# Batched x·yᵀ on one core: 2 MB stores and 64-column weight tiles, with a last tile cut into unequal partition ranges

## The chip, the cores and the metric

The kernel runs on one core of a Trainium2 chip. Its time is the device time in microseconds (us), as the median of the runs shown. The core has TensorE (PE in the profile; PEld is its weight load), VectorE (DVE), ScalarE (ACT), GpSimd (POOL), SyncE (SP, which here only issues transfers), and sixteen DMA engines that move data between the device memory and SBUF. Matrix products are written to PSUM, and an engine has to copy them to SBUF before a transfer can store them.

## The reference

```python
def setup_inputs():
    batch, n_heads, seq_t, seq_s, channels = 8, 12, 512, 512, 64
    return {
        "x": np.random.randn(batch, n_heads, seq_t, channels).astype(np.float32),
        "y": np.random.randn(batch, n_heads, seq_s, channels).astype(np.float32),
    }

def reference(x, y):
    return np.einsum('bhtc,bhsc->bhts', x, y).astype(np.float32)
```

For each of the 96 pairs of batch and head, `out = x @ y.T`: 512 x 64 times 64 x 512, in float32. The inputs are 2 x 12.6 MB and the output is 100.7 MB, so most of the traffic is the store of the output.

## The kernel before

Four heads make a group (`G = 4`), and there are `NG = 24` groups. A partition of a group holds 16 consecutive rows of one head (`R = 16`), 32 partitions a head (`Q = 32`). So a group's x or y is one contiguous block of 512 KB with 4 KB a partition, and its output is one contiguous block of 4 MB with 32 KB a partition.

`load(g)` (L48 to L53) issues the transfers of y and x for a group on SyncE's queue. Six groups are loaded ahead, and group g + 6 is asked for when group g is cast. `prepare(g)` (L61 to L93) is a generator that makes a group's operands, in four steps:

- GpSimd casts y and x to bf16 (L65, L69). y is written twice side by side, so that its transposes fill both halves of the partitions. The loads of group g + 6 are issued here.
- TensorE transposes eight blocks of y into PSUM (L78), and VectorE copies them to `yT` (L84). The copy reads PSUM with a stride, so that the columns of `yT` stand in the order of the rows of y.
- The other eight blocks follow, copied by ScalarE (L86).
- TensorE transposes x in eight blocks of two rows a partition (L90), and VectorE copies the result to `xT` as it lies (L91).

The main loop (L98 to L123) goes over the groups. For each it has eight steps k, and at every second one it takes one step of `prepare(g + 1)`. A step multiplies two rows of each partition: one PSUM tile `pm` of 128 partitions x 2 x 512, filled by eight matmuls (L109): four heads times two parities of the row (`par`). Each has 64 contraction rows and 32 weight columns, so the eight use eight separate blocks of the 128 x 128 array, two in height and four in width. ScalarE copies the even steps' `pm` to the output tile `ot` (L116), VectorE the odd ones' (L118). There are three `pm` buffers and four `ot` buffers of 4 MB.

A group's 4 MB leave in one transfer (L123), except for the first and the last group, which leave in four pieces of 1 MB (L121), each as soon as its two steps are done. All loads and stores are issued by SyncE, in the order of the program; the framework gives each a semaphore from a ring of eight. An `ot` buffer is written again only after its store has landed.

Of the kernel before, what the change touches and what calls it, by code (L numbers as in the profile page):

```python
# [1 line left out]

# [5 lines left out]


@with_exitstack  # L10
def kernel(
    ctx: ExitStack,
    tc: tile.TileContext,
    x: bass.AP,
    y: bass.AP,
    out: bass.AP,
):

    nc = tc.nc
    B, H, T, C = x.shape
    _, _, S, _ = y.shape
    P = 128
    G = 4
    Q = P // G
    R = T // Q
    NG = B * H // G
    K = R // 2
    fp32 = mybir.dt.float32  # L30
    bf16 = mybir.dt.bfloat16
    assert C * 2 == P and S == T and R == 16

    xv = x.rearrange("b h t c -> (b h t c)").rearrange("(g p n) -> g p n", p=P, n=R * C)
    yv = y.rearrange("b h t c -> (b h t c)").rearrange("(g p n) -> g p n", p=P, n=R * C)
    ov = out.rearrange("b h t s -> (b h t s)").rearrange("(g p n) -> g p n", p=P, n=R * S)

    const = ctx.enter_context(tc.tile_pool(name="const", bufs=1))
    lpool = ctx.enter_context(tc.tile_pool(name="lpool", bufs=6))
    bpool = ctx.enter_context(tc.tile_pool(name="bpool", bufs=2))  # L40
    tpool = ctx.enter_context(tc.tile_pool(name="tpool", bufs=2))
    opool = ctx.enter_context(tc.tile_pool(name="opool", bufs=4))
    ptpool = ctx.enter_context(tc.tile_pool(name="ptpsum", bufs=2, space=bass.MemoryType.PSUM))
    pmpool = ctx.enter_context(tc.tile_pool(name="pmpsum", bufs=3, space=bass.MemoryType.PSUM))

    loaded = {}

    def load(g):  # L48
        xs = lpool.tile([P, R * C], fp32)
        ys = lpool.tile([P, R * C], fp32)  # L50
        nc.sync.dma_start(ys, yv[g])
        nc.sync.dma_start(xs, xv[g])
        loaded[g] = (xs, ys)  # L53

    for g in range(6):
        load(g)

    ident = const.tile([P, P], bf16)
    make_identity(nc, ident)

    def prepare(g, made):  # L61

        xs, ys = loaded.pop(g)
        yb = bpool.tile([P, R, 2, C], bf16)
        nc.gpsimd.tensor_copy(  # L65
            yb, ys.rearrange("p (r c) -> p r c", c=C).unsqueeze(2).to_broadcast([P, R, 2, C])
        )
        xb = bpool.tile([P, R * C], bf16)
        nc.gpsimd.tensor_copy(xb, xs)  # L69
        if g + 6 < NG:  # L70
            load(g + 6)
        yield
        yT = tpool.tile([P, G * Q, R], bf16)
        xT = tpool.tile([P, K, P], bf16)
        for half in range(2):
            pt = ptpool.tile([P, K, P], bf16)
            for k in range(K):
                nc.tensor.transpose(  # L78
                    pt[:, k, :], yb[:, half * K + k].rearrange("p a c -> p (a c)"), ident
                )  # L80
            dst = yT[:, :, half * K:(half + 1) * K]
            src = pt.rearrange("p k n -> p n k")
            if half == 0:
                nc.vector.tensor_copy(dst, src)  # L84
            else:
                nc.scalar.activation(dst, src, mybir.ActivationFunctionType.Copy)  # L86
            yield
        pt = ptpool.tile([P, K, P], bf16)
        for k in range(K):
            nc.tensor.transpose(pt[:, k, :], xb[:, k * P:(k + 1) * P], ident)  # L90
        nc.vector.tensor_copy(xT, pt)  # L91
        made[g] = (xT, yT.rearrange("p n k -> p (n k)"))
        yield  # L93

    made = {}
    for _ in prepare(0, made):
        pass
    for g in range(NG):  # L98
        xT, yT = made.pop(g)
        steps = prepare(g + 1, made) if g + 1 < NG else iter(())  # L100
        ot = opool.tile([P, R, S], fp32)
        edge = g == 0 or g == NG - 1
        for k in range(K):
            if k % 2 == 0:
                next(steps, None)
            pm = pmpool.tile([P, 2, S], fp32)
            for h in range(G):
                for par in range(2):
                    nc.tensor.matmul(  # L109
                        pm[h * Q:(h + 1) * Q, par, :],  # L110
                        xT[par * C:(par + 1) * C, k, h * Q:(h + 1) * Q],
                        yT[par * C:(par + 1) * C, h * S:(h + 1) * S],
                        start=True, stop=True,
                    )
            if k % 2 == 0:
                nc.scalar.activation(ot[:, 2 * k:2 * k + 2, :], pm, mybir.ActivationFunctionType.Copy)  # L116
            else:
                nc.vector.tensor_copy(ot[:, 2 * k:2 * k + 2, :], pm)  # L118
            if edge and k % 2 == 1:
                a, b = (2 * k - 2) * S, (2 * k + 2) * S  # L120
                nc.sync.dma_start(ov[g][:, a:b], ot.rearrange("p r s -> p (r s)")[:, a:b])  # L121
        if not edge:
            nc.sync.dma_start(ov[g], ot.rearrange("p r s -> p (r s)"))  # L123


# [1 line left out]
_INS = ['x', 'y']  # L127
_OUTS = [((8, 12, 512, 512), 'float32')]


# [23 lines left out]
```

## Time and profile before

| | |
|---|---|
| Time, median of 3 runs | 309.21 us (309.09 to 309.28) |
| Profiled execution: time, span of its instructions | 309.28 us, 307.5 us |
| TensorE busy (matmuls) | 158.3 us, 51% |
| VectorE busy | 157.3 us, 51% |
| ScalarE busy | 119.1 us, 39% |
| GpSimd busy | 70.6 us, 23% |
| DMA: moved, mean rate | 126.14 MB, 410 GB/s |
| Instructions | 4865 |
| A 4 MB store, issue to landing (median) | 36.6 us |

The DMA share in the profile is the mean over the sixteen DMA engines: 1.00 when all are busy, 0.06 when one of sixteen is. Figures slightly above 1.00 come from packets whose records overlap a little at their ends. q1 is the queue that SyncE's transfers use, and q8 carries instruction code. In the answers by stretches, each engine has its busy time and, in brackets, its number of instructions. In the waits of SyncE's queue, each line has the waiting line, what ended the wait, the total in us, how many times and the longest. In the groups of instructions, the numbers after the count are the busy time in us and the mean duration in ns, then the idle time before them and what ended most of it.

The trace also has, for every transfer, sixteen landing times, one for each DMA engine that moved a part of it, without the engine's number. A 128-partition transfer is cut in sixteen parts of eight partitions, each partition's contiguous run being one packet.

### The profile page before, as it was taken

Reading aid. Unit: us, or ns where it says so; the run is one execution under the profiler, and the core shown is the slowest. Engines: PE = TensorE matmul, PEld = TensorE weight load, DVE = VectorE, ACT = ScalarE, POOL = GpSimd, SP = SyncE. Lnnn points to the kernel's source line nnn. Section 1 sums busy time; section 2 is a strip of 40 time slices with the busy share of each in tenths; the row PEclk is TensorE's granted clock in tenths of the full one; section 3 lists DMA queues with packets and bytes.
Section 4 is the critical chain, followed back from the end, with each engine's and each line's share of the span. In section 5 each row is a group of like instructions: output and inputs, shape, how many; then the busy total and the mean of one; then the engine's idle time right before and its main releaser. Section 6 shows DMA issues by size and latency. Waiting matters only on the chain.

```text
span 307.5 us, 4865 instructions
## 1 busy us (share of the span) xinstructions
PE 158.3 (51%) x2112; PEld 81.2 (26%) x2112; DVE 157.3 (51%) x144; ACT 119.1 (39%) x121; POOL 70.6 (23%) x54
## 2 busy tenths in 40 slices
PE   2877775483564735648447474383754854320000
PEld 2443342341322313224133241231413412000000
DVE  0599997275373643736537356373563775340000
ACT  1587856144162341623506336053261564330000
POOL 5863354132122221222212312132121000000000
PEclk9999998556655667575575755757555575555555
DMA  7999999999999999999999999999999999999970
GB/s 288 417 376 425 449 405 462 412 427 435 415 436 429 404 450 420 432 436 409 448 426 404 457 420 413 451 412 443 428 431 431 437 431 420 439 432 426 410 302 21
DMA packets 11253, 126.14 MB, mean 410 GB/s; under 512 B 1248, under 2 KB 1248, under 8 KB 7392
## 3 DMA queue, kind: packets, MB, share of 16 engines
q1 hardware_dynamic: 11232, 125.83, 96.7%
q8 instruction: 16, 0.26, 0.3%
q14 instruction: 5, 0.04, 0.0%
HBM read 25.17 MB, written 100.66 MB: 409 GB/s over the span
## 4 chain that ended last, share of the span: by engine, by line
DMA 72%; DVE 11%; PE 2%; issue 1%; ACT 1%; POOL 1%; SPq 0%; DVEq 0%; ACTq 0%
DMA out_dram<-ot 71%; DVE ot L118 8%; DVE yT L84 2%; PE pm L109 1%; DMA ys<-in_y_dram 1%; ACT ot L116 1%; DVE xT L91 1%; PE pt L78 1%; POOL yb L65 1%; PE pt L90 0%; ACT yT L86 0%; SPq L123 0%; DVEq L118 0%; ACTq L116 0%
## 5 line engine op out<-in xcount | busy, mean ns | idle before, releaser
L118 DVE COPY ot<-pm 128x1024 f32<-128x1024 f32 x96 | 114.8, 1221 | 91.0 <-DMA out_dram<-ot 77.2
L116 ACT ACTIVATE ot<-pm 128x1024 f32<-128x1024 f32 x96 | 96.0, 1023 | 143.9 <-DMA out_dram<-ot 121.2
L109 PE MATMUL pm<-yT,xT 64*32 64x512 bf16 x1536 | 98.0, 555 | 100.6 <-ACT ot L116 84.0
L109 PEld LDWEIGHTS <-xT 64*32 64x32 bf16 x1536 | 30.0, 96 | 156.2 <-issue 142.9
L65 POOL CAST yb<-ys 128x2048 bf16<-128x2048 f32 x24 | 45.5, 1896 | 96.9 <-DMA ys<-in_y_dram 79.6
L78 PE MATMUL pt<-ident,yb 128*128 128x128 bf16 x384 | 42.8, 278 | 7.2 <-POOL yb L65 6.1
L69 POOL CAST xb<-xs 128x1024 bf16<-128x1024 f32 x24 | 25.0, 1042 | 65.1 <-PE pt L90 65.1
L78 PEld LDWEIGHTS <-yb 128*128 128x128 bf16 x384 | 35.5, 131 | 15.5 <-issue 7.8
L84 DVE COPY yT<-pt 128x1024 bf16<-128x1024 bf16 x24 | 29.2, 1215 | 7.2 <-PE pt L78 7.2
L90 PE MATMUL pt<-ident,xb 128*128 128x128 bf16 x192 | 26.4, 284 | 5.6 <-ACT yT L86 4.9
L86 ACT ACTIVATE yT<-pt 128x1024 bf16<-128x1024 bf16 x24 | 24.5, 1019 | 8.6 <-PE pt L78 8.6
L91 DVE COPY xT<-pt 128x1024 bf16<-128x1024 bf16 x24 | 16.6, 690 | 17.5 <-PE pt L90 17.5
L90 PEld LDWEIGHTS <-xb 128*128 128x128 bf16 x192 | 16.9, 127 | 18.1 <-issue 18.1
L86 ACT ACT_TABLE_LOAD x1 | 1.3, 1283 | 0.7 <-PEq L138 0.7
masks.py:199 POOL TENSOR_SCALAR_AFFINE_SELECT ident<-ident 128x128 bf16<-128x128 bf16 x1 | 0.3, 294 | 0.1
masks.py:197 POOL MEMSET ident<- 128x128 bf16 x1 | 0.2, 205 | 0.3 <-POOLq L138 0.3
L138 POOL MEMSET const-float32-0.0<- 128x1 f32 x1 | 0.1, 99 | 0.2 <-issue 0.2
L138 POOL MEMSET const-bfloat16-1.0<- 128x1 bf16 x1 | 0.1, 102 | 0.0
L138 POOL MEMSET const-uint8-127<- 128x1 uint8 x1 | 0.1, 102 | 0.0
L138 POOL MEMSET const-float32-1.0<- 128x1 f32 x1 | 0.1, 99 | 0.0
## 6 DMA issues: line engine op xcount, KB each, us to landing
out_dram<-ot SPq DMA_DIRECT2D x22, 4096.0 KB, 36.6
ys<-in_y_dram SPq DMA_DIRECT2D x24, 512.0 KB, 35.7
xs<-in_x_dram SPq DMA_DIRECT2D x24, 512.0 KB, 27.3
out_dram<-ot SPq DMA_DIRECT2D x8, 1024.0 KB, 23.6
```

Of the source, the lines that this page charges most:

```text
L65: nc.gpsimd.tensor_copy(yb, ys.rearrange("p (r c) -> p r c", c=C).unsqueeze(2).to_broadcast([P, R, 2, C]))
L69: nc.gpsimd.tensor_copy(xb, xs)
L78: nc.tensor.transpose(pt[:, k, :], yb[:, half * K + k].rearrange("p a c -> p (a c)"), ident)
L84: nc.vector.tensor_copy(dst, src)
L86: nc.scalar.activation(dst, src, mybir.ActivationFunctionType.Copy)
L90: nc.tensor.transpose(pt[:, k, :], xb[:, k * P:(k + 1) * P], ident)
L91: nc.vector.tensor_copy(xT, pt)
L109: nc.tensor.matmul(pm[h * Q:(h + 1) * Q, par, :], xT[par * C:(par + 1) * C, k, h * Q:(h + 1) * Q], yT[par * C:(par + 1) * C, h * S:(h + 1) ...
L116: nc.scalar.activation(ot[:, 2 * k:2 * k + 2, :], pm, mybir.ActivationFunctionType.Copy)
L118: nc.vector.tensor_copy(ot[:, 2 * k:2 * k + 2, :], pm)
L138: nc = _bacc.Bacc("TRN2", target_bir_lowering=False, num_devices=1)
```

## The change

The output is split in halves of a group: `HP = 2` heads a tile, with 8 rows a partition (`I = 8`), 64 partitions a head. A tile is then 2 MB with 16 KB a partition, contiguous in the output as before. There are eight `ot` buffers of half the size, and two stores a group in place of one.

A weight tile has 64 columns in place of 32. The 64 partitions of a head are index q' = 2q + e, where q is one of the 32 partitions that the loaded x uses and e tells the first eight of its 16 rows from the last eight. To have these 64 columns side by side, the copy of the transposed x (L91) now writes `xT` with a stride of two elements, interleaving e. A `pm` takes four matmuls (two heads, two parities), and a group has 32 in place of 64. The copies of the transposed y are unchanged, and so are the number and size of the evictions.

Only the first tile and the last tile leave in pieces now. The first leaves in two pieces of 1 MB. The last is cut along the row into four ranges, and three of them are also cut along the partitions: columns of 6 KB a partition over 120 + 8 partitions, of 2 KB over all 128, of 3 KB over 108 + 20 and of 5 KB over 126 + 2, seven transfers in all.

```diff
+    HP = 2
+    I = R // 2
-    ov = out.rearrange("b h t s -> (b h t s)").rearrange("(g p n) -> g p n", p=P, n=R * S)
+    ov = out.rearrange("b h t s -> (b h t s)").rearrange("(g a p n) -> g a p n", a=G // HP, p=P, n=I * S)
...
-    opool = ctx.enter_context(tc.tile_pool(name="opool", bufs=4))
+    opool = ctx.enter_context(tc.tile_pool(name="opool", bufs=8))
...
-        xT = tpool.tile([P, K, P], bf16)
+        xT = tpool.tile([P, K // 2, P, 2], bf16)
...
-        nc.vector.tensor_copy(xT, pt)
+        nc.vector.tensor_copy(
+            xT.rearrange("p i n e -> p i e n"), pt.rearrange("p (e i) n -> p i e n", e=2)
+        )
...
-        ot = opool.tile([P, R, S], fp32)
-        edge = g == 0 or g == NG - 1
-        for k in range(K):
-            if k % 2 == 0:
-                next(steps, None)
-            pm = pmpool.tile([P, 2, S], fp32)
-            for h in range(G):
-                for par in range(2):
-                    nc.tensor.matmul(
-                        pm[h * Q:(h + 1) * Q, par, :],
-                        xT[par * C:(par + 1) * C, k, h * Q:(h + 1) * Q],
-                        yT[par * C:(par + 1) * C, h * S:(h + 1) * S],
...
+        for hp in range(G // HP):
+            ot = opool.tile([P, I, S], fp32)
+            edge = (g == 0 and hp == 0) or (g == NG - 1 and hp == 1)
+            for i2 in range(I // 2):
+                if i2 % 2 == 0:
+                    next(steps, None)
+                pm = pmpool.tile([P, 2, S], fp32)
+                for h2 in range(HP):
+                    h = hp * HP + h2
+                    for par in range(2):
+                        nc.tensor.matmul(
+                            pm[h2 * 64:(h2 + 1) * 64, par, :],
+                            xT[par * C:(par + 1) * C, i2, h * Q:(h + 1) * Q, :].rearrange("c q e -> c (q e)"),
+                            yT[par * C:(par + 1) * C, h * S:(h + 1) * S],
...
+                if edge and i2 % 2 == 1:
+                    otf = ot.rearrange("p r s -> p (r s)")
+                    if g == 0:
+                        cuts = [((2 * i2 - 2) * S, (2 * i2 + 2) * S, P)]
+                    elif i2 == 1:
+                        cuts = [(0, 3 * S, 120), (3 * S, 4 * S, P)]
+                    else:
+                        cuts = [(4 * S, 5 * S + S // 2, 108), (5 * S + S // 2, 8 * S, 126)]
+                    for a, b, n in cuts:
+                        nc.sync.dma_start(ov[g, hp][:n, a:b], otf[:n, a:b])
+                        if n < P:
+                            nc.sync.dma_start(ov[g, hp][n:, a:b], otf[n:, a:b])
+            if not edge:
+                nc.sync.dma_start(ov[g, hp], ot.rearrange("p r s -> p (r s)"))
```

## The prediction

> **What bounds the kernel now.** I read the page's slices and DMA queue first, then busy time in stretches, then the landing of every transfer on each of its sixteen DMA engines, then the queue of SyncE, and the compute groups last.
>
> The page, and its line on the queue that carries all loads and stores:
>
> ```profile
> DMA  7999999999999999999999999999999999999970
> ...
> q1 hardware_dynamic: 11232, 125.83, 96.7%
> q8 instruction: 16, 0.26, 0.3%
> ```
>
> The DMA engines are full from the second slice on, while no compute engine is above 51%. So an edit of compute is worth only what it does to the DMA engines, and what can be won lies in their 3.3% of idle time and in how evenly they end. The end, in stretches (columns: us, engines busy with instruction counts, clock, DMA share, GB/s):
>
> ```profile
> 237.20:247.40 10.20, 7.09 (x88) 3.67 (x88) 6.64 (x7) 4.90 (x5) 0.00 (x0) 0.57 1.01 432
> 257.40:267.50 10.10, 4.47 (x64) 1.25 (x64) 4.80 (x4) 3.99 (x4) 0.00 (x0) 0.50 0.99 423
> 267.50:277.40 9.90, 2.60 (x40) 0.75 (x39) 4.80 (x4) 3.99 (x4) 0.00 (x0) 0.50 1.00 431
> 277.40:287.10 9.70, 0.00 (x0) 0.00 (x0) 0.00 (x0) 0.00 (x0) 0.00 (x0) 0.50 0.98 424
> ...
> 297.00:300.20 3.20, 0.00 (x0) 0.00 (x0) 0.00 (x0) 0.00 (x0) 0.00 (x0) 0.50 0.34 143
> 300.20:306.60 6.40, 0.00 (x0) 0.00 (x0) 0.00 (x0) 0.00 (x0) 0.00 (x0) 0.50 0.06 24
> ```
>
> From 300.2 us the share is 0.06, one engine of sixteen: a single straggler holds the end for 6.4 us. The trace's landing records say the same. The last store's sixteen shares, us behind the first at 295.97:
>
> ```
> 0.00 0.01 0.05 0.46 0.54 0.73 1.38 2.55 2.87 2.95 3.04 3.43 3.61 3.74 4.13 | 10.58
> ```
>
> Their mean is 2.50. Three layers are seen in how they came about. (1) The straggler's lag grows while instructions run and stops with them: by 0.47, 0.40, 0.34, 0.25 and 0.00 us in the windows from 237.2, 247.4, 257.4, 267.5 and 277.4, in which all engines and sequencers together ran 193, 161, 139, 100 and 0 instructions: 2.46 ns an instruction each time, and hardly at all while only loads ran. (2) The q8 packets, TensorE's code, each put one engine back by about 1.45 us in one step (2.83 to 4.27 between the stores landing from 142.8 and 155.0). Sixteen of them make the eight engines at 2.55 to 4.13. (3) The rest is below 0.9.
>
> SyncE's queue and the compute groups:
>
> ```profile
> SPq L52 <- DMA out_dram<-ot: 130.1, 15, 9.9
> ...
> L118 DVE COPY ot<-pm 128x1024 f32<-128x1024 f32 x96 | 114.8, 1221 | 91.0 <-DMA out_dram<-ot 77.2
> L109 PE MATMUL pm<-yT,xT 64*32 64x512 bf16 x1536 | 98.0, 555 | 100.6 <-ACT ot L116 84.0
> ...
> L84 DVE COPY yT<-pt 128x1024 bf16<-128x1024 bf16 x24 | 29.2, 1215 | 7.2 <-PE pt L78 7.2
> ...
> L91 DVE COPY xT<-pt 128x1024 bf16<-128x1024 bf16 x24 | 16.6, 690 | 17.5 <-PE pt L90 17.5
> ...
> out_dram<-ot SPq DMA_DIRECT2D x22, 4096.0 KB, 36.6
> ```
>
> Evictions wait for stores to land (77.2 us on VectorE), not the reverse. SyncE waits at the loads because a transfer is issued only once the one eight before it has landed (the load at 199.37 waits for the store issued at 162.68, landed at 199.31).
>
> **The change, part by part.** A group costs an engine 9.67 us for the 4 MB store (its fastest landings go 266.81, 276.48) and 1.23 each for the loads: 12.1 us.
>
> Smaller stores. A 1 MB piece takes 2.45 us of an engine (288.62, 291.07, 293.53, 295.97), so four cost 9.80 against 9.67: a further transfer costs (9.80 - 9.67)/3 = 0.04, and a KB (9.67 - 0.04)/256 = 0.0376. A 2 MB store is 128 x 0.0376 + 0.04 = 4.85. Before: 22 x 9.67 + 8 x 2.45 = 232.3. After: 46 x 4.85 + 2 x 2.45 + the last tile (4.81 + about five transfers x 0.04) = 233.0. Plus 0.7 on every engine; packet records (309 ns for 8 KB, 1213 for 32 KB) give at most 1.4, and 0 is the other end.
>
> Half the matmuls. A group goes from 64 matmuls and weight loads to 32 of each: 2 x 768 fewer in 24 groups, 3329 instructions for 4865. After 25 us, where the lag grows, about 1370 fall away: 1370 x 2.46 = 3.4 us off the straggler. The ends are 0 (the lag goes by time or by bytes) and 3.4; I take 3.4, because five windows with different counts and equal lengths lie on one line. Of code, TensorE has 2688 instructions for 4224, so 16 x 2688/4224 = 10 fetches: six of the eight twice-hit engines come forward by 1.45.
>
> TensorE's time. One pm tile takes eight matmuls in 0.51 us (24 in 1.54 at 149.89), each 604, so they overlap; four of twice the columns take between 0.51 and 4 x 0.604 = 2.4. I take 0.51, the row of the same tile. A group is then 8 x 0.51 + 2.9 of transposes (42.8 + 26.4, by 24) = 7.0 us under 12.1.
>
> The strided x copy. From 690 towards the strided 1215 of L84: plus 0.53 x 24 = 12.6 us on VectorE, per group 4 x 1.22 + 1.22 + 1.22 = 7.3 of 12.1. At the start it delays the first store from 14.91 to some 15.4, while loads land until 25.75. Nothing; with that cover gone, 0.5.
>
> Waits on SyncE. With four transfers a group, eight in flight are two groups, 24 us, in place of 32; the straggler's lag (at most 10.6) leaves an engine over 13 us queued. Behind a blocked issue stand the next stores, and behind those only evictions. The last tile's 126-row store waits for the landing of the tile three back, on the straggler two tiles and 16 KB (10.4 us) ahead of its end, near 289; the others have work until 296. Nothing.
>
> The last tile. It has 2 MB, 128 KB an engine when even. The trace has only 128 rows over sixteen engines, eight each. If a row count goes over as many engines as divide it, always the same first ones, then 120, 108 and 126 rows go over 15, 12 and 14, and 8, 20 and 2 over 8, 10 and 2. Summed at 6, 2, 3 and 5 KB a row:
>
> ```
> engine    0-1  2-7  8-9  10-11  12-13  14  15
> KB        153  148  142  136    109    64  16
> ```
>
> The Trainium skill, DMA: Bandwidth & Descriptors, "Why a DMA increments its semaphore by 16 and not by 1", states this rule (the largest count up to 16 that divides the slowest dimension, lowest-numbered engines), which no run here shows.
>
> If engine 15 is the straggler, it is relieved of 112 x 0.0376 = 4.2 us; were it among the first two, it gains 0.9. For the cost of transfers under 128 rows I have only bounds: 0, as for the 8 KB pieces, or the last tile's 148 KB at half rate, 4.8 us more. I take 0.3, near the pieces, since no transfer here runs slower for being small.
>
> The same page's "Rules for kernel authors" asks for 128 partitions and at least 1 MiB a transfer for full bandwidth, and speaks against this tile; our 1 MB pieces at 2.45 us are within 1.3% of full rate with a queue behind them. By the rule I would charge these pieces something like the upper bound and forecast about 308.
>
> **Sum.** Straggler, relieved: 306.54 + 0.7 - 3.4 - 4.2 = 299.6. A once-hit engine at the old worst place: 295.97 + 0.7 + (4.13 - 1.45) + 20 x 0.0376 + 0.2 for the extra transfers = 300.3, which is last (a twice-hit one without relief: 301.7). With 0.3: 300.6. The old span ended 0.97 after its last landing, and the profiled execution took 309.28 against the span's 307.51, 1.77 more; the median of the three runs, 309.21, is 0.07 under it. 300.6 + 0.97 + 1.77 = 303.3.
>
> **Rivals.**
> Straggler not relieved: it sits among the first engines. 306.54 + 0.7 - 3.4 + 0.9 = 304.8, so 307.5. For it: the records do not number the engines. Against: one odd engine of sixteen is likelier at an end of the row, and one end is relieved. The same page ("Latency and other measured facts") calls 7 and 15 usually slower, with a reason that does not apply to SyncE's queue; it would halve the chance.
>
> Lag not tied to instructions, relieved: 306.54 + 0.7 - 4.2 = 303.0, so 305.8. Against it stand the five windows. With no relief either, 308.1 and 310.9.
>
> Slower, by an uneven split: a row count that is no power of two goes over fewer engines, 120 over 8 (15 rows each), 108 over 4 (27), 126 over 2 (63). The busiest engine then carries 90 + 6 + 16 + 81 + 15 + 315 + 5 = 528 KB, 400 more than even: 15.0 us; 296.7 + 15.0 + up to 2.7 gives 314.5 to 317, say 316. It decides for slower once one engine gets 7 us, 190 KB, too much. For it: no row shows such a transfer. Against: 128 rows are cut in whole rows evenly.
>
> TensorE becomes the bound: four matmuls of a pm one after another, 8 x 2.4 + 2.9 = 22 us a group, over 500 in all. It decides at (12.1 - 2.9)/8 = 1.15 us a pm. Against: eight tiles overlap now on the same halves of the rows.
>
> **How the numbers follow.** Relieved and shorter, 303.3: 0.66. Not relieved, 307.5: 0.17. Lag stays, relieved, 305.8: 0.08. Both fail, 310.9: 0.04. Uneven split, 316: 0.03. TensorE: 0.02. Faster by over 0.2% (about what a measurement of this kernel can tell from no change) 0.90, within it 0.02 (not relieved, with a costlier last tile), slower 0.08. The likeliest case alone runs from 301.7, near an even end (mean lag 2.5 less 0.75, at 298.4, is 301.2), to 305. The range goes on to the unrelieved case: 301.7 to 307.7.
>
> **What would show it.** In the profile after: about 10 q8 packets; MATMUL 64*64 x768 with a pm still near 0.5 us; L91's copy near 1215 ns; 2 MB stores 4.85 us apart on one engine; no stretch at 0.06 share for over 2 us. The prediction is wrong if that stretch stays, if the last tile's transfers take longer than their bytes, or if the DMA share falls below 0.97 between 25 and 270 us.

## The result, and the profile after

The changed kernel takes 311.82 us (311.36 to 312.27, 4 runs) against 309.15 (308.98 to 309.28): a ratio of 1.0087, 95% interval 1.0069 to 1.0104. It is slower by 0.9%, where 303.3 was forecast, and outside the range. The profiled execution took 312.08 us, and its span is 309.9. The ratios here and below leave disturbed runs out, so where a kernel's runs spread, its ratio can lie on the other side of 1 from its median, which is taken over all runs.

The page's lines on the DMA engines and queues, for the kernel after:

```profile
DMA  7999999999999999999999999999999999999960
...
q1 hardware_dynamic: 14413, 125.84, 96.9%
q8 instruction: 10, 0.16, 0.2%
```

The middle is as before: full, and TensorE's code takes 10 fetches for 16. The same page's groups of the matmuls and the x copy:

```profile
L116 PE MATMUL pm<-yT,xT 64*64 64x512 bf16 x768 | 96.3, 566 | 89.0 <-ACT ot L123 71.3
...
L94 DVE COPY xT<-pt 128x1024 bf16<-128x1024 bf16 x24 | 31.1, 1298 | 9.5 <-PE pt L93 9.5
```

A matmul of 64 columns takes 566 ns on average, where one of 32 took 555, and they still overlap: twelve, which is three `pm`, take 1.55 us from 148.58, so 0.52 a `pm`. The x copy went to 1298 ns. Neither shows in the time: the first experiment keeps both and is faster than the kernel before. What is new lies at the end, in stretches (DMA share and GB/s are the last two columns):

```profile
286.00:291.00 5.00, 0.00 (x0) 0.00 (x0) 0.00 (x0) 0.00 (x0) 0.00 (x0) 0.50 1.01 433
...
294.00:296.00 2.00, 0.00 (x0) 0.00 (x0) 0.00 (x0) 0.00 (x0) 0.00 (x0) 0.50 0.99 281
296.00:298.00 2.00, 0.00 (x0) 0.00 (x0) 0.00 (x0) 0.00 (x0) 0.00 (x0) 0.50 0.87 240
298.00:300.00 2.00, 0.00 (x0) 0.00 (x0) 0.00 (x0) 0.00 (x0) 0.00 (x0) 0.50 0.60 198
...
304.00:309.00 5.00, 0.00 (x0) 0.00 (x0) 0.00 (x0) 0.00 (x0) 0.00 (x0) 0.50 0.06 23
```

From 294 to 296 us the engines are 0.99 busy and move 281 GB/s, where the same share moved 433 before the engines came to the cut tile. And one engine is alone for the last 5 us, as before the change. The landing records of the last transfers of after follow, in us behind the first record of each. A transfer on fewer than sixteen engines has one record more than it has shares; it comes 0.4 to 0.5 us after the issue, and the times of these transfers count from it.

```
the 2 MB store but one        286.91: ... 3.59 3.88 3.91 |  7.51
the last 2 MB store           291.78: ... 3.86 3.89 4.23 | 11.18
120 rows, 15 shares           267.09: ... 30.87 31.95 33.76 | 37.91
8 rows, 8 shares              270.57: ... 25.15 25.48 27.30 | 34.66
128 rows, 16 shares           292.90: ... 5.70 7.25 8.61 | 12.96
108 rows, 12 shares           280.35: ... 19.32 19.64 22.21 | 26.61
20 rows, 10 shares            285.15: ... 14.75 15.10 | 22.06
126 rows, 14 shares           290.09: ... 12.53 14.21 | 18.84  (lands at 308.93)
2 rows, 2 shares              294.83: 3.07 4.98
```

Three readings follow. The numbers of shares are 15, 8, 16, 12, 10, 14 and 2, as the prediction assumed and as the Trainium skill's rule has it (DMA: Bandwidth & Descriptors, "Why a DMA increments its semaphore by 16 and not by 1"). The straggler's lag stood at 7.5 us, 3.1 less than before, so this gain came. In the last whole store, where the other engines have gone on to the cut tile, it jumps to 11.2: 3.7 us are lost there. And the straggler is not relieved. Behind its last whole store (302.96) its shares land at 305.00, 305.22, 305.86, 306.97, 307.22 and 308.93: after 305.00 the steps are 0.23, 0.64, 1.10, 0.25 and 1.72 us, near what 6, 16, 27, 6 and 45 KB take at 0.0376 us a KB. So it has a share of each transfer but the 2-row store, and no idle time between them. If transfers take the lowest-numbered engines, it is one of the third to the eighth, which carry 148 KB of the last tile.

The packet records of the trace show where the 3.7 us went. The six 16 KB packets that start after 295.19 us follow one another without overlap, so they are of one engine, the straggler at its last whole store. They take 2616, 1232, 1327, 616, 611 and 1022 ns, where 611 is usual: 3.76 us over. In the even end of the experiments (e9_even_third) none of the 63 such packets from 291 us on takes more than 640. Nor are the small packets of the cut tile slow as a rule: half of the 6 KB ones take 234 ns or less, but single ones up to 1801.

### The profile page after: what moved, and what is told of

Read it like the earlier page. It is cut to its first block, busy times and chain, and to the rows that moved or that the text cites. A ratio compares the mean times of both kernels' runs of the same rounds, so it can differ in the third digit from the quotient of the medians.

```text
span 309.9 us, 3414 instructions
## 1 busy us (share of the span) xinstructions
PE 154.4 (50%) x1344; PEld 81.7 (26%) x1344; DVE 172.7 (56%) x144; ACT 117.5 (38%) x121; POOL 70.6 (23%) x54
## 4 chain that ended last, share of the span: by engine, by line
DMA 70%; DVE 10%; PE 3%; issue 2%; ACT 1%; POOL 1%; SPq 0%; ACTq 0%
DMA out_dram<-ot 69%; DVE ot L125 7%; DVE xT L94 2%; PE pm L116 2%; DVE yT L87 1%; DMA ys<-in_y_dram 1%; ACT ot L123 1%; PE pt L81 1%; POOL yb L68 1%; PE pt L93 0%; SPq L139 0%; ACTq L123 0%
## 5 line engine op out<-in xcount | busy, mean ns | idle before, releaser
L125 DVE COPY ot<-pm 128x1024 f32<-128x1024 f32 x96 | 116.3, 1220 | 78.9 <-DMA out_dram<-ot 59.0
L123 ACT ACTIVATE ot<-pm 128x1024 f32<-128x1024 f32 x96 | 94.4, 1022 | 141.8 <-DMA out_dram<-ot 129.6
L116 PE MATMUL pm<-yT,xT 64*64 64x512 bf16 x768 | 96.3, 566 | 89.0 <-ACT ot L123 71.3
L116 PEld LDWEIGHTS <-xT 64*64 64x64 bf16 x768 | 32.1, 122 | 136.6 <-issue 118.6
L81 PE MATMUL pt<-ident,yb 128*128 128x128 bf16 x384 | 41.5, 269 | 17.6 <-DVE xT L94 11.2
L81 PEld LDWEIGHTS <-yb 128*128 128x128 bf16 x384 | 33.4, 125 | 25.7 <-issue 19.6
L94 DVE COPY xT<-pt 128x1024 bf16<-128x1024 bf16 x24 | 31.1, 1298 | 9.5 <-PE pt L93 9.5
L93 PE MATMUL pt<-ident,xb 128*128 128x128 bf16 x192 | 25.1, 286 | 5.9 <-ACT yT L89 4.5
```

The lines of the kernel that those rows point to most:

```text
L81: nc.tensor.transpose(pt[:, k, :], yb[:, half * K + k].rearrange("p a c -> p (a c)"), ident)
L94: nc.vector.tensor_copy(xT.rearrange("p i n e -> p i e n"), pt.rearrange("p (e i) n -> p i e n", e=2))
L116: nc.tensor.matmul(pm[h2 * 64:(h2 + 1) * 64, par, :], xT[par * C:(par + 1) * C, i2, h * Q:(h + 1) * Q, :].rearrange("c q e -> c (q e)"), y ...
L123: nc.scalar.activation(ot[:, 2 * i2:2 * i2 + 2, :], pm, mybir.ActivationFunctionType.Copy)
L125: nc.vector.tensor_copy(ot[:, 2 * i2:2 * i2 + 2, :], pm)
```

## The experiments

"Even end" below is the changed kernel with its last tile whole. "Straggler" is the engine whose lag climbs steadily with the instructions; in some executions of the even end another engine lags more.

**The last tile whole.** The cut is undone, the rest of the change stays.

```diff
-                    if g == 0:
-                        cuts = [((2 * i2 - 2) * S, (2 * i2 + 2) * S, P)]
-                    elif i2 == 1:
-                        cuts = [(0, 3 * S, 120), (3 * S, 4 * S, P)]
-                    else:
-                        cuts = [(4 * S, 5 * S + S // 2, 108), (5 * S + S // 2, 8 * S, 126)]
+                    cuts = [((2 * i2 - 2) * S, (2 * i2 + 2) * S, P)]
```

> The changed kernel with its last tile stored as the first one is: two pieces of 1 MB over all 128 partitions. Theory (the cut of the last tile costs the straggling engine 0.75 us of extra bytes and some 3.7 us while the cut transfers of the other engines run beside its own store): the straggler ends the last whole store at 291.8 + 7.5 = 299.3, two pieces of 2.45 follow, last landing near 304.2, time near 306.9, faster than both kernels. Rival (the loss lies in the smaller stores or the wider weight tiles, not in the cut): the time stays near 311.5.

Measured: 307.09 us (306.75 to 309.99, 7 runs) against 309.19; ratio 0.9926 (0.9913 to 0.9940). Five of the seven runs lie between 306.75 and 307.23. So the cut was the loss, and without it the change was faster here than the kernel before. The same kernel was measured twice more. Beside the changed kernel on one chip:

> The even end a third time, beside the changed kernel on the same chip: 2 to 5 us under it if the cut of the last tile costs what the landings say (0.75 and 3.7 us); equal to it if the loss lies elsewhere.

> The changed kernel as it is, on the chip of the other three: 311.4 to 312.3 as before, with the straggler's lag growing by 3 to 4 us in the last whole store.

The even end took 306.95 us (306.77 to 308.64; 0.9933, 0.9911 to 0.9955) and the changed kernel 311.75 (311.31 to 314.05; 1.0091, 1.0058 to 1.0124): 4.8 us apart, where the landings give 0.75 + 3.7. The changed kernel's straggler again went from 7.55 to 11.13 us of lag in the last whole store. The even end's stretches beside those of after:

```profile
294.00:296.00 2.00, 0.00 (x0) 0.00 (x0) 0.00 (x0) 0.00 (x0) 0.00 (x0) 0.50 1.00 422
296.00:298.00 2.00, 0.00 (x0) 0.00 (x0) 0.00 (x0) 0.00 (x0) 0.00 (x0) 0.50 0.66 279
...
304.00:309.00 5.00, 0.00 (x0) 0.00 (x0) 0.00 (x0) 0.00 (x0) 0.00 (x0) 0.68 0.00 2
```

422 GB/s at a share of 1.00 where the cut had 281 at 0.99, and nothing is left after 305.

> The even end once more, on the same chip as the other two of this call, so that they can be compared with it: 306.9 if the cut was the loss, as in the run before.

On a third chip it was less clean: a median of 310.44 us, above the 309.18 of the kernel before, with five runs from 306.75 to 309.51 and five from 311.37 to 313.06; ratio 0.9955 (0.9929 to 0.9981). That spread is taken up below.

**The cut alone, in the kernel before.** The last 2 MB of the last group leave in the change's seven transfers.

```diff
-                nc.sync.dma_start(ov[g][:, a:b], ot.rearrange("p r s -> p (r s)")[:, a:b])
+                otf = ot.rearrange("p r s -> p (r s)")
+                if g == 0 or k < 4:
+                    cuts = [(a, b, P)]
+                elif k == 5:
+                    cuts = [(a, a + 3 * S, 120), (a + 3 * S, b, P)]
+                else:
+                    cuts = [(a, a + S + S // 2, 108), (a + S + S // 2, b, 126)]
+                for a, b, n in cuts:
+                    nc.sync.dma_start(ov[g][:n, a:b], otf[:n, a:b])
+                    if n < P:
+                        nc.sync.dma_start(ov[g][n:, a:b], otf[n:, a:b])
```

> The kernel before, with the last 2 MB of its last group cut by partitions as in the change (120+8, 128, 108+20, 126+2), nothing else changed. Theory (extra bytes and a slowed neighbour): 309.2 + 0.75 + 3.7, near 313.5, and the straggler lags the first engine by more than 12 us at the end of the pieces ahead of the cut. Rival A (only the extra bytes count): 310.0. Rival B (the cut relieves the straggler): 305 to 306.

Measured: 313.74 us (313.30 to 314.40), ratio 1.0147 (1.0131 to 1.0162): 4.55 us slower than before, against the 4.45 expected. The straggler's lag in the pieces ahead of the cut was 13.3 and 13.7 us, where it had been 10.6. The cut costs nearly the same in both kernels (4.55 and 4.8 us), so it doesn't hang on the smaller stores or the weight tiles.

**Equal bytes, half the partitions at a time.** The last tile goes as 64 + 64 partitions, so every engine has as much as with 128. This line stands in place of the seven that the even end takes out.

```diff
+                    cuts = [((2 * i2 - 2) * S, (2 * i2 + 2) * S, P if g == 0 else 64)]
```

> The changed kernel with its last tile in pieces of 64 + 64 partitions: every engine has the same bytes as with 128, only the partitions that run at the same time change. If the cut's price is a place that engines share when a transfer does not span all 128 partitions: the DMA share stays near 1 between 292 and 298 us while the rate falls well below 400 GB/s, and the time is 1 to 5 us over the even end, 308 to 312. If the price is only the unequal bytes: as the even end, 306.9 to 307.2.

Measured: 310.39 us (308.96 to 314.39), ratio 1.0040 (1.0019 to 1.0062), 3.3 us over the even end on the same chip, 307.09; the traced run took 313.01. Its stretches:

```profile
294.00:296.00 2.00, 0.00 (x0) 0.00 (x0) 0.00 (x0) 0.00 (x0) 0.00 (x0) 0.50 0.95 254
296.00:298.00 2.00, 0.00 (x0) 0.00 (x0) 0.00 (x0) 0.00 (x0) 0.00 (x0) 0.50 0.89 303
298.00:300.00 2.00, 0.00 (x0) 0.00 (x0) 0.00 (x0) 0.00 (x0) 0.00 (x0) 0.50 0.71 201
```

The engines are 0.95 busy at 254 GB/s with equal bytes (429 at a share of 1.00 from 286 to 291 us), so unequal bytes alone are not what slows them; the 8 KB packets take 402 ns on average where they took 309. Whole stores suffer too: of their 67 packets of 16 KB from 291 us on, 13 take 981 to 1501 ns. The last engine's lag goes from 9.56 to 13.47 over the two last whole stores, while the others are at the halves. Here this is not the straggler, which stays at 7.14. So the cut slows packets of some engines and not of others, those of an uncut store among them, and what the two kinds of cut have in common is that a transfer spans fewer than 128 partitions. The Trainium skill has a reason that fits, SBUF — State Buffer, "Door 1: The DMA port swizzle": 64 partitions reach 8 of 16 ports. It gives 8 x 27.2 = 218 GB/s for them, and the rates of the first two stretches, with some engines still in whole stores, lie between that and full. That the shared place is a port is the page's account. The runs show that packets are held up, and don't tell the reading side in SBUF from the writing side in device memory.

**Where the straggler sits.** One range of 3 KB a partition goes as 119 + 9 rows, on seven and nine engines. Again the lines stand in place of those of the cut.

```diff
+                    if g == 0 or i2 == 1:
+                        cuts = [((2 * i2 - 2) * S, (2 * i2 + 2) * S, P)]
+                    else:
+                        cuts = [(4 * S, 5 * S + S // 2, 119), (5 * S + S // 2, 8 * S, P)]
```

> The changed kernel with an even end except for one range of 3 KB a partition, which goes as 119 + 9 partitions: seven and nine engines, 51 KB more or less. It asks where the straggler sits. If it is the eighth engine: the seven landings of the 119-row store lie within 5 us of each other, the late one is among the nine, and it carries 107 KB in place of 128, 0.8 us less: 306 to 307, if the cut's own price is small. If it is one of the first seven: one of the seven landings comes over 5 us after the rest, it carries 158 KB, and the time is near 308 or above.

Measured: 309.11 us (308.20 to 310.44; ratio 1.0001, 0.9985 to 1.0018), 2.0 over the even end. My test of "5 us after the rest" was badly set, since five engines lag here, and the last of them is not the straggler. The straggler's lag can be followed from store to store: 3.60 us at 113.68, 5.15 at 179.66, 7.29 at 291.75. An engine at 8.24 has stood there since 187 us.

The packet records tell the five apart in the piece ahead of the cut range. The engine that has lagged at 8.24 ends that piece last (landing at 303.29) and goes on at once with 5 KB packets, so it is in neither part of the range. The one before it (302.01) then sends seventeen packets of 3 KB, five of them in 176 to 792 ns where the others take 121, and is the last of the seven to land, at 305.88. The straggler landed the piece at 301.47, and 51 KB take 1.96 us, which fits the landing of the seven at 303.43. So it is one of the first seven, and by the 2-row store of after not of the first two: the third to the seventh engine. This assumes that the numbering is in order and that the straggler is the same engine in both executions.

**Does the straggler's lag go by instructions?** Two attempts first made another engine the bound.

```diff
+                for _ in range(4):
+                    nc.scalar.activation(tick[:, 0:1], tick[:, 1:2], mybir.ActivationFunctionType.Copy)
```

> The changed kernel with an even end, and four one-column copies on ScalarE added to every step: 768 instructions that move almost no data and are no part of the result. If the straggler's lag goes by instructions of any engine (2.46 ns each): its lag before the last tile grows from 7.5 to about 9.4 us and the time is 1.9 over the even end, near 308.8. If the lag goes by matmuls, weight loads or TensorE's code alone: lag 7.5 and the time of the even end, 306.9.

Measured: 340.22 us (1.0994, 1.0972 to 1.1016). The page:

```profile
L129 ACT ACTIVATE tick<-tick 128x1 f32<-128x1 f32 x768 | 155.7, 203 | 22.7
```

A copy of one column takes 203 ns, 6.5 us a group, which ScalarE did not have: its busy share went to 78% and the DMA queue's fell to 90.3%. The run says nothing on the lag. The same with `nc.gpsimd.memset(tick, 0.0)`:

> The changed kernel with an even end, and four fills of two columns on GpSimd added to every step: 768 instructions of about 0.1 us that are no part of the result (GpSimd was 23% busy, so that it does not become the bound as ScalarE did). If the straggler's lag goes by instructions of any engine (2.46 ns each): 1.9 us more lag before the last tile, 9.4 for 7.5, and 1.9 us over the even end of the same call. If it goes by TensorE's instructions alone: the lag and the time of the even end.

Measured: 313.10 us (1.0122, 1.0099 to 1.0145). The fills wait for nothing, and so stood ahead of the casts and delayed them; the rate fell to 259 GB/s at about 160 us, and all lags shrank as the queue ran empty, to 0.24 us at most in the store landing from 171.1. Again no answer. On VectorE, with `nc.vector.memset(tick, 0.0)`, they stand between evictions:

> The even end, and four fills of two columns on VectorE (some 60 ns each) added to every step: 768 instructions that are no part of the result and add 0.24 us a step to an engine busy 56% of the time. In the changed kernel and in the even ends one engine's lag grows by 0.025 us each us from 125 to 260 us, where the program runs about 11.5 instructions a us (2.2 ns each). If it goes by instructions of any engine: 3 more instructions a us, 0.032 us each us, about 1.9 us more lag at the end. If it goes by TensorE's instructions alone: 0.025 as before. The time is of less use: from 306.8 to 309 by either, because of the spread of the even end.

```profile
L128 DVE MEMSET tick<- 128x2 f32 x768 | 46.1, 60 | 45.0 <-PEq L152 0.8
```

The DMA engines stayed full. Counted from the third engine in order, the steadily climbing lag went from 5.26 us in the store landing from 155.4 to 8.47 in that from 243.3, while some 1370 instructions ran: 2.34 ns each, 0.037 us a us. In the changed kernel the same lag went from 3.27 (108.9) to 5.80 (206.6) in 1128 instructions: 2.24 ns each, 0.026 a us. Two executions without the fills, those of the halves and of the 119 + 9 rows, gave 0.025 and 0.026 from 155 to 243 us, counted from the first engine. So the lag goes by the instructions of VectorE too. Before its last tile the straggler stood at 9.1 us, where the 7.5 of the changed kernel and 768 x 2.46 ns give 9.4. The time, 309.16 us (ratio 1.0014, 0.9994 to 1.0034), says little beside the spread of the even end.

**The price of smaller stores, and the spread.**

```diff
-            nc.sync.dma_start(ov[g], ot.rearrange("p r s -> p (r s)"))
+            otf = ot.rearrange("p r s -> p (r s)")
+            for a in (0, K * S):
+                nc.sync.dma_start(ov[g][:, a:a + K * S], otf[:, a:a + K * S])
```

> The kernel before with each whole store of a group cut in two of 16 KB a partition, all else as it was. By the landings of before a further transfer costs an engine 0.04 us: 22 x 0.04 = 0.9, so 310.0 to 310.1. Rival A (runs of 16 KB cost nothing): 309.2. Rival B (they are dear, and are what made the changed kernel slow): 311 or above.

Measured: 310.81 us (310.40 to 311.89), ratio 1.0052 (1.0034 to 1.0069): 1.6 us more, not 0.9. In its profile, of the slowest run, the first engine ends 1.27 later than in before (297.24), and the last one lags by 11.72. Small, and no cause of the result, but nearly twice my estimate; these runs lie 32 KB apart in memory, which those of the change don't.

> The changed kernel with one store of 4 MB a group (two runs of 16 KB a partition) in four buffers of 4 MB, and the last group in four pieces of 1 MB over 128 partitions: three transfers a group in place of four, as before the change, with the wider weight tiles and the shorter runs kept. If the spread between runs of the even end (306.75 to 313) comes from the number of transfers in flight: 306.5 to 307 in every run. If it comes from the shorter runs in memory: the spread stays.

The edit keeps both halves of a group in one buffer of 32 KB a partition and stores them once; of its lines, the store:

```diff
+            nc.sync.dma_start(ov[g].rearrange("a p n -> p a n"), both.rearrange("p a r s -> p a (r s)"))
```

Measured: 309.57 us, 306.34 to 311.59; ratio 0.9969 (0.9937 to 1.0001). The spread stays with three transfers a group, so their number is not its cause. In the profiles of the even ends, engines other than the straggler lag by 4 to 12 us in their own right, gained mostly between 60 and 160 us; in the two of the changed kernel, none by over 4.2 ahead of the last whole store. What gives rise to that, and why it differs between executions, is open. The run says the spread goes along with the 16 KB runs or the layout that brings them, and no more.

## Why the prediction was wrong

**The bound, right.** The DMA engines and the one that ends last decide; in the change no compute engine became the bound.

**Smaller stores, right.** 0.7 was the term. The last whole store first lands at 291.78; before, the same point is 295.97 less the last 2 MB (4.9), at 291.07. With 22 further transfers in the kernel before, though, 1.6 us came where 0.9 was expected.

**Half the instructions, right.** Lag 7.5 us where 7.2 follows from the terms, and 10 fetches. This is the gain that the even end keeps: 307 us in place of 309.2, on two chips of three.

**TensorE, the copy, SyncE: right,** all hidden.

**The last tile, wrong in two steps.** The first is the place of the straggler. "One odd engine of sixteen is likelier at an end of the row" had nothing behind it but symmetry, and 0.66 went to it. The rival that it isn't relieved, 307.5, was the true case of the two, with the 148 KB of the table. The second is the term for transfers under 128 rows: bounds of 0 and 4.8, of which I took 0.3, "since no transfer here runs slower for being small"; it measured 3.7. The nearest row was chosen by the wrong likeness. The 8 KB pieces are small, but they span 128 partitions. The span is what the cuts that cost time share, and of that the trace had no row at all. So the middle of the bounds, or both ends as cases of their own, was the honest choice. I also charged the term to the transfers that are cut, on engines that had room; the 3.7 us fell on the straggler's own whole store, which is not cut. Unrelieved, 304.8, plus 3.7 makes 308.5 for the last landing, which came at 308.93; the time lies 3.15 above that. The Trainium skill's rule of 128 partitions (DMA: Bandwidth & Descriptors, "Rules for kernel authors"), weighed and set aside, pointed the right way. That the 308 worked out by it came nearer than 303.3 is in part luck, since it still took the straggler as relieved.

The range fails with them: its upper end was the unrelieved case with the cheap transfer, and the two mishaps together were given no case. (Of its chances, the three slower cases add up to 0.09, where the summary has 0.08.)

## What to carry to other kernels

When one DMA engine ends late, first see what makes it late, and cut that; here halving TensorE's instructions gave 2 us and needed no knowledge of the engine. To shift bytes from engine to engine by cutting a tile along its partitions, you must know which engine is late, and the cut is not free: while transfers that span fewer than 128 partitions ran, the engines moved 281 GB/s for 433, and 254 for 429, at nearly the same busy share, and an engine still at an uncut store lost 3.7 us. The change with its last tile whole took 307 us on two chips, less than both kernels; on a third its median was 310.4, so the gain of 2 us is not safe.

## What the runs showed that was not expected

One DMA engine of sixteen loses 2.2 to 2.5 ns for each instruction, counted over all engines, while stores go on: shown by windows of before, by the change's smaller count and by 768 added fills on VectorE. For ScalarE and GpSimd by themselves it is not shown. Why it is that engine, the runs don't show. All executions on record carry the profiler's span and clock, and its record notes each instruction; whether the engine would lag as much without that recording is open too. A fetch of 16 KB of TensorE's code sets one engine back by 1.45 us, and a one-column copy on ScalarE costs 203 ns against 60 for a fill on VectorE and 99 on GpSimd.
